# Output and gate weight pairs made beside the late convolution tiles, norm sums taken later, first squares queued behind the copies

## The chip, the cores and the metric

The kernel runs on one core of a Trainium2 chip. Five engines work side by side, each through its own queue in order: TensorE (PE, with PEld for its weight loads), VectorE (DVE), ScalarE (ACT), GpSimd (POOL), and SyncE (SP), which here issues nearly all transfers. The metric is the device time of one execution in microseconds; lower is better.

## The reference, cut to what matters

One layer over 2048 positions of width 1024, all in float32, and a final norm:

```python
h = rmsnorm(x, norm_g)
c_b, c_c, c_h, c_z, q, k, v, a_z = split(h @ w_in)         # 1024 x 4096
y_c = c_b * causal_dwconv(c_c * c_h, conv_w, conv_b)        # three taps
y_a = stick_breaking_attention(q, k, v)                     # 8 heads of 64
y = group_rmsnorm(concat(y_c, y_a)) * silu(concat(c_z, a_z))
x = x + y @ w_out                                           # 1024 x 1024
gate = sigmoid(rmsnorm(x, ple_norm_g) @ w_pg + b_pg)        # 1024 x 1024
x = x + gate * (p @ w_pe)
out = rmsnorm(x, final_g)
```

Stick-breaking attention takes, for a row of scores z, sigmoid(z) times the running product of sigmoid(-z) over the keys between key and query.

## The kernel before

The sequence lies in four chunks of 512 positions, c = 3, 2, 1, 0 (reversed, so chunk 3 needs no other). A weight tile is 128 output channels by 1024 inputs: eight blocks kt of 128x128, in two halves f of 128x512. Every float32 operand is split into a high part (a cast to the fast matmul type) and a low part (the rest), and a product is three matmuls: high by high, high by low, low by high (`product`, L283 to L285).

**Weights.** A half is either raw or a pair. A raw half is loaded into one of two `wr` buffers (`fetch_w`, L252, which loads as far ahead as the two buffers allow), cast on ACT to `wh` (L269), and the rest is taken on POOL as `wl` (L270). A half that another pass will need is then stored as a pair in DRAM (`store_w`, L277), and the later pass loads the pair (L266) with no work on ACT or POOL. Which halves are pairs is said by `paired`, which are stored by `kept`. The 16 output and gate tiles (`OUT0` and up) are raw and stored in the pass of chunk 3, pairs in those of chunks 2 and 1, and raw again in that of chunk 0.

**Order.** The program is traced in this order: the start (`first_tile` of tiles 24 and 16, for chunks 3 and 2, with the split of x and the first two norms); E, the projections of chunks 3 and 2; L, the projections of chunks 1 and 0 (q, k, v and attention gates first, then the convolution tiles c, h, b and g); `work2`, the last convolution tile with its gate; then for each chunk an output stage (`out_stage`, 8 tiles) and a gate stage (`gate_stage`, 8 tiles). A step is one `product`. Beside the steps runs `attention()`, pulled at a set rate per step (0.64 in E, 0.86 in L, 0.72 in the stages after), and generators called `besides`, one `next` per step: `norm_later`, `y_prep`, `final`, and `pe_pairs`, which splits and stores the eight tiles of w_pe. `later(n, f)` calls f n steps on. A scheduler then orders each engine's queue, so that work which it takes to be ready early can be issued ahead of what was traced before it; `tc.issue_after(ins)` holds what a block puts on the engine of `ins` behind `ins` in that queue, and no other engine's.

**Norms.** A norm is: squares summed over eight tiles into `acc`; `norm_r`, matmuls of `acc` by ones into `ssp` (L177); a DVE instruction (L183); a power on POOL (L185); then `norm_spread`, transposes into `rT` (L195) and a copy `rB` (L197) by which results are multiplied. At the start `first_squares` squares tiles 2, 4 and 6 and sums them on POOL (L206, L208), squares the others on ACT (L212), and the sums of these are DVE additions (L215). After a stage `out_stage` calls `norm_of` 6 steps on and `norm_spread` 10 steps on; `final` waits 8 steps, then calls `norm_of`, and 8 more before `norm_spread`.

**Attention.** A row: scores `z` (L535, L536), two ACT sigmoids (L538, L540), a DVE scan (L554, L557), a product on DVE or POOL in turn (L564), transposes `tp` (L603), a cast `ah` on ACT (L606), the rest `al` on DVE (L611), and two matmuls into `av` (L574, L575).

Single buffers that matter here (`BUFS`): `sh`, `sl` and `acc` have one each. PSUM tag `mm` has two banks, which the projections and stages share.

Of the kernel before, what the change touches and what calls it, by code (L numbers as in the profile page):

```python
# [14 lines left out]
P = 128  # L15
# [18 lines left out]
def build(tc, xt_d, pt_d, wst_d, wpe_d, cst_d, out_d):  # L34
# [5 lines left out]
    with ctx:  # L40
# [108 lines left out]

        latest = [None]  # L150

# [4 lines left out]
        def scaled_split(key, kt, xt, gain, lag=0):  # L156
            hh, hl = pair(key, kt)
            nc.scalar.activation(hh, xt, AF.Copy, scale=gain)

            def low():  # L160
                nc.vector.scalar_tensor_tensor(  # L161
                    out=hl, in0=xt, scalar=gain, in1=hh.bitcast(F32), op0=ALU.mult, op1=ALU.subtract)
                note()
            if lag:
                later(lag, low)
            else:
                low()
# [13 lines left out]
        def norm_sum(slot, ssp):  # L181
            r, r2 = rr[:, 8 * slot:8 * slot + 4], rr[:, 8 * slot + 4:8 * slot + 8]
            nc.vector.tensor_scalar(out=r, in0=ssp[:, 0:8:2], scalar1=1.0 / DM, scalar2=EPS,  # L183
                                    op0=ALU.mult, op1=ALU.add)
            nc.gpsimd.tensor_tensor(out=r, in0=r, in1=nhalf[:, 0:4], op=ALU.pow)  # L185
            if slot < 4:
                nc.vector.scalar_tensor_tensor(out=r2, in0=r, scalar=1.0 / HD, in1=r, op0=ALU.mult,
                                               op1=ALU.mult)
# [48 lines left out]
        def paired(t, tag):  # L237

            return tag[1] in (1, 2) if t >= OUT0 else tag == 1

        def kept(t, tag):
            return tag[1] == 3 if t >= OUT0 else tag == 3

        def fetch_w():

            while len(raws) < RAWS and fetched[0] < 2 * len(wq):
                t, tag = wq[fetched[0] // 2]
                f = fetched[0] % 2
                fetched[0] += 1
                if not paired(t, tag):  # L250
                    raw = pj.tile([P, CH], F32, tag="wr", bufs=RAWS, name=f"wr{t}_{made[0]}")
                    nc.sync.dma_start(raw, wst_d[t, f])  # L252
                    raws.append(raw)
# [33 lines left out]
        def proj(t, chunks, evac, besides=(None, None)):  # L287

            tag = chunks[0]
            for i, c in enumerate(chunks):  # L290
                pp = bank("mm", 2, f"pp{t}_{c}")
                for kt in range(KT):
# [7 lines left out]
                    yield  # L300
                if i and besides[i] is not None:
                    for _ in besides[i]:
                        pass
# [154 lines left out]

        def conv_c(ct, chunks):
            def evac(c, pp):  # L460
                cc[c] = buf("cc", f"cc{ct}_{c}")
                nc.vector.tensor_tensor(out=cc[c], in0=pp, in1=rB[c], op=ALU.mult)
                nc.gpsimd.tensor_tensor(out=cc[c], in0=cc[c], in1=rB[c], op=ALU.mult)

            return proj(4 + ct, chunks, evac)

        def conv_h(ct, chunks):
            def evac(c, pp):
# [17 lines left out]

            return proj(8 + ct, chunks, evac)

# [6 lines left out]

        def conv_b(ct, chunks):
            return proj(ct, chunks, evac_b(ct))

# [224 lines left out]
        def out_stage(c, besides=None):  # L723
# [26 lines left out]
            if besides is not None:  # L750
                for _ in besides:
                    yield
            later(6, norm_of, slot, ("x1", c))
            later(10, norm_spread, slot)

# [129 lines left out]
        def final(c):  # L885

            for _ in range(8):
                yield
# [64 lines left out]
        def pairs_of(chunks, order, last=None, first_besides=None):  # L953
# [3 lines left out]
            for n, (kind, i) in enumerate(order):  # L957
                besides = (first_besides if n == 0 else None, last if n == len(order) - 1 else None)
                if kind in kinds:
                    t0, f = kinds[kind]  # L960
                    args = (i, chunks) + ((besides,) if kind in "qv" else ())
                    add(work, f, *args, tiles=[(t0 + i, chunks[0])])
                else:
                    t, gi = (12 + i, i) if kind == "g" else (28 + i, 4 + i)
                    b = besides
                    if chunks == cE and (kind, i) in (("g", 1), ("g", 2)):
                        b = (norm_later(cL[i - 1]),) * 2
                    if chunks == cL and (kind, i) in (("g", 0), ("g", 1)):
                        b = (pairs_e,) * 2
# [28 lines left out]

        wq.extend([(24, cE[0]), (16, cE[0])])
        workE = pairs_of(cE, orderE, last=ahead(splits(1), 2))  # L1000
        pairs_e = pe_pairs()
        workL = pairs_of(cL, orderL[:-2], first_besides=ahead(splits(0), 2))
# [36 lines left out]
        split_w(att, ("ah", "al"))  # L1039
        adds3, acc3 = first_squares(3, x3)  # L1040
        for kt in range(KT):
            x_split(2, kt, x2[kt])
            if kt == 5:
                behind_first = latest[0]
        with tc.issue_after(behind_first):
            for f in adds3:
                f()
        first_tile(16, 3)
        norm_r(3, acc3)
        adds2, acc2 = first_squares(2, x2)  # L1050
        split_w()

        def beside_first(kt):
            if kt == 4:
                norm_spread(3)
            if kt == 6:
                evacs[24](3, pps[24, 3])
                evacs[16](3, pps[16, 3])
                tick()
        first_tile(24, 2, beside_first)  # L1060
        for f in adds2:
            f()
        split_w()
        first_tile(16, 2, lambda kt: tick() if kt in (2, 4, 6) else None)
        norm_r(2, acc2)
# [20 lines left out]
        for c in (3, 2, 1, 0):  # L1086
# [5 lines left out]
            def gates(c=c):  # L1092
                return gate_stage(c, y_prep(c - 1) if c else None)
            add(tail[-1], gates, need=[(h, c - 1) for h in range(NH)] if c else [],
                tiles=[(GATE0 + m, ("x1", c)) for m in range(KT)])
        run(workL, RATE_L)
        run(work2, RATE_Y)
        for work in tail[:3]:
# [70 lines left out]
```

## Time and profile before

| | |
|---|---|
| median of 3 runs | 1659.58 us (1654.53 to 1660.13) |
| the profiled execution | 1655.82 us, span 1654.1 us |
| mean granted TensorE clock | 0.981 |
| busy share | PE 96%, PEld 78%, DVE 69%, ACT 48%, POOL 46% |
| DMA | 333.99 MB, 202 GB/s over the span |

The span is from the first to the last instruction. The stages lie at: start 0 to about 62 us, E to 498, L to about 1025 (its convolution tiles from about 790), `work2` to 1058, output and gate stage of chunk 3 to about 1225, of chunk 2 to about 1420, of chunk 1 to about 1540, of chunk 0 to the end. A granted clock of 1 is full speed, 0.5 is half. A busy PE is modelled from pipelined matmuls, so a stage is judged by how much of it PE is not busy and by the clock it was granted.

### The profile page before, as it was taken

The page shows a single profiled execution, that of the slowest core. Times are in us where ns is not written, and L with a number is a line of the kernel's source. Part 1 is how long each engine was busy: PE and PEld are TensorE (multiplying, and loading weights), DVE is VectorE, ACT ScalarE, POOL GpSimd, SP SyncE. Part 2 cuts the span into 40 slices and gives each one's busy share as a digit, 9 for nine tenths or more (in the row PEclk, how much of TensorE's full clock was granted, in tenths as well). Part 3 has the DMA queues.
Part 4 walks back from the last instruction along what each step waited for, and adds up shares of the span by engine and source line. Part 5 has one row for each costly group of instructions (what it writes and reads, how often), then busy time and mean ns, then how long its engine had stood idle before and what let it go on. Part 6 is the DMA issues. An engine that isn't in the chain of part 4 may idle for free.

```text
span 1654.1 us, 23295 instructions
## 1 busy us (share of the span) xinstructions
PE 1589.9 (96%) x7622; PEld 1288.5 (78%) x7622; DVE 1145.1 (69%) x1475; ACT 796.8 (48%) x1574; POOL 757.8 (46%) x711
## 2 busy tenths in 40 slices
PE   7899999999999999999999999988999999999996
PEld 5778787887888788888888888767777777877885
DVE  6475677776655767666777777778877876854544
ACT  5344454554434545545444454456555454543453
POOL 7444545454460423223433432767664355424542
PEclk9899999999999999999999999998999999999998
DMA  6666766848547655556743333587877866868742
GB/s 215 196 213 187 242 200 204 263 136 255 196 160 230 203 149 186 160 182 193 230 136 110 125 117 108 162 278 268 281 262 259 282 225 229 277 201 289 246 133 89
DMA packets 184712, 333.99 MB, mean 202 GB/s; under 512 B 21776, under 2 KB 22800, under 8 KB 184592
## 3 DMA queue, kind: packets, MB, share of 16 engines
q1 hardware_dynamic: 181712, 327.27, 61.4%
q10 hardware_dynamic: 2880, 5.24, 0.9%
q8 instruction: 60, 0.98, 0.3%
q14 instruction: 60, 0.49, 0.1%
HBM read 217.08 MB, written 115.34 MB: 201 GB/s over the span
## 4 chain that ended last, share of the span: by engine, by line
PE 55%; DVE 5%; DMA 5%; POOL 4%; issue 3%; ACT 3%; SPq 1%; DVEq 0%; ACTq 0%; POOLq 0%
PE pp L283 8%; PE pp L284 8%; PE pp L285 8%; PE tp L603 4%; PE px L283 3%; PE px L285 3%; PE px L284 3%; PE z L535 2%; PE z L536 2%; PE av L575 2%; PE av L574 2%; PE py L283 2%; PE py L284 2%; PE py L285 2%; DVE T L557 2%
## 5 line engine op out<-in xcount | busy, mean ns | idle before, releaser
L283 PE MATMUL pp<-hhh,wh 128*128 128x512 f32 x1008 | 404.6, 401 | 0.0
L284 PE MATMUL pp<-hhl,wh 128*128 128x512 f32 x1008 | 398.5, 395 | 3.7 <-DVE hhl L161 3.6
L285 PE MATMUL pp<-hhh,wl 128*128 128x512 f32 x1008 | 397.1, 394 | 0.0
L557 DVE TENSOR_TENSOR_SCAN T<-s,carry,small 128x513 f32<-128x513 f32 x192 | 287.8, 1500 | 124.7 <-ACT s L538 116.5
L538 ACT ACTIVATE s<-z 128x512 f32<-128x512 f32 (+1 forms) x320 | 171.6, 536 | 272.3 <-PE z L536 269.9
L564 POOL TENSOR_TENSOR b<-b,T 128x512 f32<-128x512 f32 (+1 forms) x160 | 199.1, 1245 | 154.0 <-DVE T L557 66.9
L611 DVE TENSOR_TENSOR al<-tp,ah 128x512 fp32r<-128x512 f32 (+1 forms) x320 | 190.9, 597 | 46.1 <-ACT ah L606 45.6
L284 PEld LDWEIGHTS pp<-hhl,wh 128*128 128x128 f32 x1008 | 190.4, 189 | 41.5 <-DVE hhl L161 6.6
L285 PEld LDWEIGHTS pp<-hhh,wl 128*128 128x128 f32 x1008 | 189.9, 188 | 42.2
L270 POOL TENSOR_TENSOR wl<-wr,wh 128x512 fp32r<-128x512 f32 x126 | 178.7, 1420 | 95.7 <-ACT wh L269 85.4
L562 POOL COPY carry<-T 128x1 f32<-128x1 f32 x192 | 53.6, 279 | 363.4 <-DVE T L554 184.4
L283 PEld LDWEIGHTS pp<-hhh,wh 128*128 128x128 f32 x1008 | 190.3, 189 | 36.3 <-issue 1.0
L606 ACT CAST ah<-tp 128x512 fp32r<-128x512 f32 (+1 forms) x320 | 168.0, 526 | 83.9 <-PE tp L603 80.0
L603 PE MATMUL tp<-first,b 128*128 128x128 f32 x1088 | 174.5, 275 | 7.0 <-POOL b L564 3.8
L554 DVE TENSOR_TENSOR_SCAN T<-s,first 128x513 f32<-128x513 f32 (+3 forms) x128 | 125.5, 989 | 75.1 <-ACT s L538 71.7
L603 PEld LDWEIGHTS tp<-first,b 128*128 128x128 f32 x1088 | 138.4, 142 | 49.4 <-POOL b L564 4.8
L540 ACT ACTIVATE b<-z 128x512 f32<-128x512 f32 (+1 forms) x320 | 170.2, 532 | 0.0
L574 PE MATMUL av<-ah,vv 128*128 128x512 f32 (+1 forms) x320 | 140.8, 440 | 5.1 <-ACT ya L584 3.3
L564 DVE TENSOR_TENSOR b<-b,T 128x512 f32<-128x512 f32 (+2 forms) x160 | 131.4, 821 | 12.2 <-ACT ah L606 0.5
L535 PE MATMUL z<-kk,q 128*128 128x512 f32 (+1 forms) x320 | 119.7, 374 | 8.5 <-DMA kk<-qk_d 5.2
L269 ACT CAST wh<-wr 128x512 fp32r<-128x512 f32 x126 | 78.7, 624 | 88.7 <-DMA wr<-in_wst_dram 33.0
L575 PE MATMUL av<-al,vv 128*128 128x512 f32 (+1 forms) x320 | 118.9, 372 | 0.2 <-DVE al L611 0.2
(167 smaller groups left out, 2659.0 us busy)
## 6 DMA issues: line engine op xcount, KB each, us to landing
wr<-in_wst_dram SPq DMA_DIRECT2D x128, 256.0 KB, 3.1
wh<-wp_d SPq DMA_DIRECT2D x128, 256.0 KB, 3.1
wl<-wp_d SPq DMA_DIRECT2D x128, 256.0 KB, 3.5
wp_d<-wh SPq DMA_DIRECT2D x94, 256.0 KB, 3.4
wp_d<-wl SPq DMA_DIRECT2D x94, 256.0 KB, 3.6
kk<-qk_d SPq DMA_DIRECT2D x80, 256.0 KB, 4.2
vv<-v_d SPq DMA_DIRECT2D x80, 256.0 KB, 3.6
q<-qk_d SPq DMA_DIRECT2D x64, 256.0 KB, 4.3
```

Of the source, the lines that this page charges most:

```text
L270: nc.gpsimd.tensor_tensor(out=wl, in0=raw, in1=wh.bitcast(F32), op=ALU.subtract)
L283: nc.tensor.matmul(pp, wh[:, sl], hh, start=(kt == 0), stop=False)
L284: nc.tensor.matmul(pp, wh[:, sl], hl, start=False, stop=False)
L285: nc.tensor.matmul(pp, wl[:, sl], hh, start=False, stop=(kt == KT - 1))
L538: nc.scalar.activation(s[:, 1:w + 1], zp[:, 0:w], AF.Sigmoid, scale=-0.125)
L540: nc.scalar.activation(bt[:, 0:w], zp[:, 0:w], AF.Sigmoid, scale=0.125)
L557: nc.vector.tensor_tensor_scan(T[:, 0:w + 1], s[:, 0:w + 1], zeros.to_broadcast([P, w + 1]), carries[h, qc][:, j:j + 1], op0=ALU.mult, op1 ...
L564: return lambda: eng.tensor_tensor(out=bt[:, 0:w], in0=bt[:, 0:w], in1=T[:, 0:w], op=ALU.mult)
L574: nc.tensor.matmul(av[:, 0:w], v[:, kb], ah[:, 0:w], start=diag and kb == 3, stop=False)
L603: nc.tensor.transpose(tp[:, j * P:(j + 1) * P], bt[:, kb * P - k0:(kb + 1) * P - k0], ident)
L606: nc.scalar.copy(ah[:, 0:w], tp[:, 0:w])
L611: nc.vector.tensor_tensor(out=al[:, 0:w], in0=tp[:, 0:w], in1=ah[:, 0:w].bitcast(F32), op=ALU.subtract)
```

## The change

- `weight_pairs`, a new generator, makes all 32 halves of the output and gate tiles into pairs: it loads a raw half into `wr`, casts it into `sh` on ACT two steps on, takes the rest into `acc` on POOL, stores both four steps later, and yields once more, so that a half takes seven steps. It runs beside the 14 convolution and convolution gate tiles of L (224 steps). The output and gate tiles of chunks 3, 2 and 1 are then loaded as pairs; chunk 0's stay raw; none is stored in a stage. It runs on from tile to tile instead of being emptied at a tile's end, and what is left after L is drained.
- `pe_pairs` moves from the convolution gates 0 and 1 to the attention gates 1 and 2 of L, and also runs on.
- `fetch_w` looks no further than three halves past the last one made.
- `out_stage`: `norm_of` after 8 steps (was 6), `norm_spread` after 13 (was 10). `final`: 11 steps (was 8).
- The start: `first_squares(3)` is traced after the splits of chunk 2 and its ACT part queued behind the third of these copies; `norm_r(3)` comes six steps later, inside tile 24 of chunk 2; the POOL part of `first_squares(2)` is queued behind the power of norm 3; `norm_spread(3)` and the evacuations of chunk 3 move into tile 16 of chunk 2.

```diff
         def paired(t, tag):
-            return tag[1] in (1, 2) if t >= OUT0 else tag == 1
+            return tag[1] > 0 if t >= OUT0 else tag == 1
         def kept(t, tag):
-            return tag[1] == 3 if t >= OUT0 else tag == 3
+            return t < OUT0 and tag == 3
+        def weight_pairs():
+            for t in range(OUT0, OUT0 + 2 * KT):
+                for f in range(2):
+                    raw = pj.tile([P, CH], F32, tag="wr", bufs=RAWS, name=f"wr{t}_p{f}")
+                    nc.sync.dma_start(raw, wst_d[t, f])
+                    for _ in range(2):
+                        yield
+                    wh, wl = buf("sh", f"wh{t}_p{f}", F32R), buf("acc", f"wl{t}_p{f}", F32R)
+                    nc.scalar.copy(wh, raw)
+                    nc.gpsimd.tensor_tensor(out=wl, in0=raw, in1=wh.bitcast(F32), op=ALU.subtract)
+                    for _ in range(4):
+                        yield
+                    store_w(t, f, wh, wl)
+                    yield
         def fetch_w():
-            while len(raws) < RAWS and fetched[0] < 2 * len(wq):
+            while len(raws) < RAWS and fetched[0] < min(2 * len(wq), made[0] + 3):
...
-                if i and besides[i] is not None:
+                if i and besides[i] not in (None, pairs_w, pairs_e):
                     for _ in besides[i]:
                         pass
...
-            later(6, norm_of, slot, ("x1", c))
-            later(10, norm_spread, slot)
+            later(8, norm_of, slot, ("x1", c))
+            later(13, norm_spread, slot)
...
         def final(c):
-            for _ in range(8):
+            for _ in range(11):
                 yield
             norm_of(8 + c, ("o", c))
...
+                    if chunks == cL and kind in "chb":
+                        besides = (pairs_w,) * 2
+                    add(work, f, i, chunks, besides, tiles=[(t0 + i, chunks[0])])
...
-                    if chunks == cL and (kind, i) in (("g", 0), ("g", 1)):
+                    if chunks == cL and kind == "g":
+                        b = (pairs_w,) * 2
+                    if chunks == cL and kind == "a" and i in (1, 2):
                         b = (pairs_e,) * 2
...
-        adds3, acc3 = first_squares(3, x3)
         for kt in range(KT):
             x_split(2, kt, x2[kt])
+            if kt == 2:
+                copied = latest[1]
             if kt == 5:
                 behind_first = latest[0]
+        with tc.issue_after(copied):
+            adds3, acc3 = first_squares(3, x3)
         with tc.issue_after(behind_first):
             for f in adds3:
                 f()
         first_tile(16, 3)
-        norm_r(3, acc3)
-        adds2, acc2 = first_squares(2, x2)
-        split_w()
+        adds2 = []
         def beside_first(kt):
-            if kt == 4:
+            if kt == 5:
+                norm_r(3, acc3)
+                power = latest[2]
+                with tc.issue_after(power):
+                    adds2.extend(first_squares(2, x2))
+                split_w()
+        first_tile(24, 2, beside_first)
+        adds2, acc2 = adds2
+        def beside_second(kt):
+            if kt == 2:
                 norm_spread(3)
-            if kt == 6:
+            if kt == 3:
                 evacs[24](3, pps[24, 3])
                 evacs[16](3, pps[16, 3])
+                for f in adds2:
+                    f()
+                split_w()
+            if kt > 4:
                 tick()
-        first_tile(24, 2, beside_first)
-        for f in adds2:
-            f()
-        split_w()
-        first_tile(16, 2, lambda kt: tick() if kt in (2, 4, 6) else None)
+        first_tile(16, 2, beside_second)
         norm_r(2, acc2)
...
         run(workL, RATE_L)
+        for g in (pairs_e, pairs_w):
+            for _ in g:
+                tick()
```

`latest[1]` is set to the ACT copy in `scaled_split`, `latest[2]` to the POOL power in `norm_sum`; `conv_c`, `conv_h` and `conv_b` pass `besides` on to `proj`.

## Rows read from the trace of the kernel before

**Rows 1.** Page, part 1: busy us, share of the span, instructions
```profile
PE 1589.9 (96%) x7622; PEld 1288.5 (78%) x7622; DVE 1145.1 (69%) x1475; ACT 796.8 (48%) x1574; POOL 757.8 (46%) x711
```

**Rows 2.** Windows by stage: busy us (instructions), clock, DMA share, GB/s
```profile
core 0: us, PE busy (x) PEld busy (x) DVE busy (x) ACT busy (x) POOL busy (x), PEclk, DMA share, GB/s
100.00:498.00 398.00, 393.28 (x1954) 325.43 (x1953) 271.60 (x366) 189.43 (x399) 203.59 (x168) 1.00 0.64 204
498.00:790.00 292.00, 288.74 (x1435) 237.29 (x1434) 198.63 (x263) 143.62 (x288) 83.67 (x103) 1.00 0.61 188
...
830.00:1058.00 228.00, 227.76 (x1120) 184.90 (x1120) 171.55 (x232) 107.59 (x212) 93.26 (x99) 1.00 0.37 118
1058.00:1225.00 167.00, 153.74 (x696) 119.80 (x695) 134.16 (x141) 92.50 (x180) 123.53 (x102) 0.95 0.80 267
1225.00:1420.00 195.00, 186.68 (x886) 149.69 (x886) 149.94 (x182) 100.26 (x198) 84.86 (x85) 0.97 0.76 252
```

**Rows 3.** Windows of the start, columns as in rows 2
```profile
7.30:18.30 11.00, 7.34 (x26) 3.96 (x25) 10.62 (x9) 11.00 (x20) 10.00 (x7) 1.00 0.97 356
...
30.80:47.20 16.40, 7.87 (x24) 6.29 (x25) 7.57 (x8) 3.54 (x6) 13.53 (x16) 0.59 0.44 160
```

**Rows 4.** Timeline of PE in the start: start, us, [idle before <-releaser]
```profile
34.22 1.87 PE L177 MATMUL ssp<-small,xsq 128*128 128x2 f32 x8 [3.45 <-DVE xsq L215]
...
43.54 1.12 PE L195 MATMUL rT<-first,rr 128*128 128x128 f32 x4 [5.11 <-POOL rr L185]
```

**Rows 5.** Timeline of DVE in the start
```profile
36.13 0.16 DVE L183 TENSOR_SCALAR rr<-ssp 128x4 f32<-128x4 f32 x1 [0.29 <-PE ssp L177]
```

**Rows 6.** Timeline of POOL in the start
```profile
25.09 4.50 POOL L206 TENSOR_TENSOR xsq<-xf 128x512 f32<-128x512 f32 x1 [4.54 <-DVE xsq L215]
29.66 1.28 POOL L208 TENSOR_TENSOR xsq<-xsq,xsq 128x512 f32<-128x512 f32 x1
...
42.46 1.03 POOL L185 TENSOR_TENSOR rr<-rr,small 128x4 f32<-128x4 f32 x1
```

**Rows 7.** POOL by line, 1058 to 1225: busy us, mean ns | idle before
```profile
L270 POOL TENSOR_TENSOR wl<-wr,wh 128x512 fp32r<-128x512 f32 x30 | 45.6, 1521 | 8.4 <-ACT wh L269 8.4
```

**Rows 8.** ACT by line, 1058 to 1225
```profile
L269 ACT CAST wh<-wr 128x512 fp32r<-128x512 f32 x29 | 18.2, 627 | 16.1 <-DMA wr<-in_wst_dram 14.5 <-PE px L284 1.0 <-PE py L284 0.5
```

**Rows 9.** Waits of SP's queue, 1058 to 1225: us, times, longest
```profile
SPq L252 <- POOL wl L270: 42.2, 20, 5.8
```

**Rows 10.** Waits of PE, 1058 to 1250
```profile
PE ssp L177 <- POOL acc L717: 3.6, 2, 2.2
...
PE z L535 <- ACT b L540: 3.2, 2, 2.9
...
PE av L574 <- ACT ah L606: 1.7, 1, 1.7
```

**Rows 11.** Waits of PE, whole span
```profile
PE ssp L177 <- POOL acc L717: 7.5, 6, 2.6
```

**Rows 12.** Tiles py and px, high matmuls: first and last start
```profile
L283 PE MATMUL py<-yhh,wh x256: 387/390/796, 1058.3 to 1581.0; 128*128 128x512 f32 x128
...
L283 PE MATMUL px<-x1hh,wh x256: 387/392/774, 1139.4 to 1637.4; 128*128 128x512 f32 x128
```

**Rows 13.** DVE by line, 830 to 1058
```profile
L557 DVE TENSOR_TENSOR_SCAN T<-s,carry,small 128x513 f32<-128x513 f32 x43 | 62.6, 1456 | 33.9 <-ACT s L538 30.1 <-POOL b L564 2.6 <-POOL carry L562 0.6
...
L564 DVE TENSOR_TENSOR b<-b,T 128x512 f32<-128x512 f32 (+2 forms) x29 | 19.3, 664 | 2.1 <-ACT ah L606 0.5
```

**Rows 14.** DVE by line, 1058 to 1225
```profile
L557 DVE TENSOR_TENSOR_SCAN T<-s,carry,small 128x513 f32<-128x513 f32 x24 | 41.7, 1738 | 8.8 <-ACT s L538 8.8
...
L564 DVE TENSOR_TENSOR b<-b,T 128x512 f32<-128x512 f32 (+2 forms) x16 | 18.0, 1123 | 0.9
```

**Rows 15.** Window in chunk 1's output stage, columns as in rows 2
```profile
1425.00:1450.00 25.00, 25.00 (x122) 20.51 (x121) 23.57 (x29) 14.12 (x28) 9.53 (x12) 1.00 0.93 309
```

**Rows 16.** Waits of SP's queue, 830 to 1058
```profile
SPq L266 <- PE pp L285: 67.4, 22, 9.7
```

**Rows 17.** Page, part 6: transfers, KB each, us to landing
```profile
wp_d<-wh SPq DMA_DIRECT2D x94, 256.0 KB, 3.4
```

More of the change, by code (lines that the diff above doesn't have):

```diff
@@ L148, in load @@
             return t
-        latest = [None]
+        latest = [None] * 3
         def note():
@@ L158, in scaled_split @@
             nc.scalar.activation(hh, xt, AF.Copy, scale=gain)
+            latest[1] = nc.cur_bb.bb.instructions[-1]
             def low():
@@ L185, in norm_sum @@
             nc.gpsimd.tensor_tensor(out=r, in0=r, in1=nhalf[:, 0:4], op=ALU.pow)
+            latest[2] = nc.cur_bb.bb.instructions[-1]
             if slot < 4:
@@ L457, in build, with conv_c @@
         cc = {}
-        def conv_c(ct, chunks):
+        def conv_c(ct, chunks, besides=(None, None)):
             def evac(c, pp):
@@ L463, in evac, with conv_h @@
                 nc.gpsimd.tensor_tensor(out=cc[c], in0=cc[c], in1=rB[c], op=ALU.mult)
-            return proj(4 + ct, chunks, evac)
-        def conv_h(ct, chunks):
+            return proj(4 + ct, chunks, evac, besides)
+        def conv_h(ct, chunks, besides=(None, None)):
             def evac(c, pp):
@@ L485, in tap @@
                     op0=ALU.mult, op1=ALU.add)
-            return proj(8 + ct, chunks, evac)
+            return proj(8 + ct, chunks, evac, besides)
         def evac_b(ct):
@@ L494, in evac_b, with conv_b @@
             return evac
-        def conv_b(ct, chunks):
-            return proj(ct, chunks, evac_b(ct))
+        def conv_b(ct, chunks, besides=(None, None)):
+            return proj(ct, chunks, evac_b(ct), besides)
         jobs = [(h, c) for h in range(NH) for c in (3, 2)] + [(h, c) for c in (1, 0) for h in range(NH)]
@@ L960, in pairs_of @@
                     t0, f = kinds[kind]
-                    args = (i, chunks) + ((besides,) if kind in "qv" else ())
-                    add(work, f, *args, tiles=[(t0 + i, chunks[0])])
+                    if chunks == cL and kind in "chb":
+                        besides = (pairs_w,) * 2
+                    add(work, f, i, chunks, besides, tiles=[(t0 + i, chunks[0])])
                 else:
@@ L999, in build @@
         wq.extend([(24, cE[0]), (16, cE[0])])
+        pairs_e, pairs_w = pe_pairs(), weight_pairs()
         workE = pairs_of(cE, orderE, last=ahead(splits(1), 2))
-        pairs_e = pe_pairs()
         workL = pairs_of(cL, orderL[:-2], first_besides=ahead(splits(0), 2))
```

## The prediction

> **What bounds the kernel now.** I read the page first: PE is busy for 1589.9 us and no other engine comes near [rows 1]. So the kernel can only lose time where PE stands or runs at half clock, and the question is where that happens. Windows by stage answer it [rows 2]. I count a stage's loss as its length less PE's busy time, plus the busy time multiplied by one minus the granted clock. E loses 398 - 393.28 = 4.7 us, the first part of L 3.3, the late convolution tiles 0.2. Chunk 3's stages lose 13.3 standing and 153.74 x 0.05 = 7.7 by the clock, 20.9 in 167 us; chunk 2's lose 8.3 + 5.6 = 13.9 in 195. In the start, 30.80 to 47.20 loses 8.5 standing and 7.87 x 0.41 = 3.2 by the clock: 11.8 [rows 3]. Then the waits say what PE stood for: in the start for a sum of squares (3.45) and for the spread of the first norm (5.11), released by POOL's power [rows 4]; behind the stages for `acc` [rows 10, 11], and in chunk 3 for ACT.
>
> The clock here has two levels, 1.2 and 2.4 GHz, and a window mean of 0.59 is a mix of them. In each stage with a mean below 1 PE had stood for microseconds just before, so a stall costs more than its own length.
>
> **The change part by part.** The sum is made against the profiled execution, 1655.82 us, whose span is 1654.1; the median shown is 3.8 higher, within the spread of the three runs (5.6).
>
> *Squares behind the copies (ACT).* From 7.3 to 18.3 PE stands 3.7 us. ACT is busy all of it, but DVE too for 10.62 of 11.00 [rows 3], so copies that come sooner find DVE full of low parts. Nothing, with 3.7 gained and 1 lost (squares later than the additions that need them) as ends.
>
> *The first norm.* It now comes inside tile 24 of chunk 2, and only POOL's squares of chunk 2 are held behind its power. Before, the DVE step was over at 36.29, and the power ran at 42.46 [rows 5, 6]: 6.2 of the 8.5 us came from POOL's order alone, as POOL was then on other work (13.53 of 16.40 busy [rows 3]). The other 3.45 came from DVE's order, where a sum for chunk 3 stood behind additions for chunk 2; these are now traced after it. Upper end 11.8 gained. Lower end: the second norm becomes late instead. POOL's three squares and two sums for chunk 2 can't start before the power; at the undisturbed 1.28 us of one [rows 6] they are 6.4 us, so PE may stand some 6 us more in front of the second sum. I take **-8**, nearest to 6.2 and its share of the half clock (6.2/8.5 x 11.8 = 8.6).
>
> *Weight pairs, in chunk 3's stages.* 32 casts of 627 ns (20.1 us of ACT) and 32 subtractions of 1521 ns (48.7 us of POOL) leave [rows 7, 8], with 32 raw loads and 64 stores; 64 loads of pairs come. What the raw halves hold up is seen in two queues. SP stands 42.2 us at `wr` loads that wait for POOL to free a buffer [rows 9], and every transfer behind waits with them; ACT stands 14.5 us in front of casts whose half has not landed [rows 8], and the sigmoids and casts of attention stand behind. Two of PE's waits, for `ah` (1.7) and for a bank that ACT empties (3.2), follow these directly: 4.9, the lower end [rows 10]. For the upper end chunk 2's stages serve, which load pairs already: of their 13.9 lost, 2.2 [rows 10] and at most the rest of the sums' 7.5 [rows 11], 3.9, are norm waits, and the 5.6 of half clock I give to these; 2.2 are left, 1.9 for 167 us. Chunk 3, less its own norm wait of 1.4, would gain 20.9 - 1.4 - 1.9 = 17.6. I take the middle: **-11**. DVE profits too: its product took 1123 ns there against 664 in the late convolution tiles, its scan 1738 against 1456 [rows 13, 14].
>
> *Weight pairs, beside the late convolution tiles.* The same 32 casts, subtractions and 96 transfers now fall into a stretch that loses 0.2 us. POOL goes from 93.26 to some 142 of 228 us (62%), ACT from 107.59 to 128 [rows 2]. If DVE's 43 scans and 29 products stretched as far as in chunk 3's stages, that is 43 x 0.28 + 29 x 0.46 = 25 us, DVE at 197 of 228 (86%); a window with DVE at 94% had PE full [rows 15], so this is covered. SP is the weaker point: it already stands up to 9.7 us at pair loads waiting for PE [rows 16]. The stores and raw loads now queue there, and with one `sh` buffer the next cast waits for the store, 3.4 us to land [rows 17], three steps after its issue. Of steps of 1.27 us in chunk 3 (64 from 1058.3 to 1139.4 [rows 12]) that is 3.8: no margin when SP is blocked. Behind a waiting cast stand the sigmoids, and behind them DVE's scan and PE's transposes. Bounds: E, which makes raw halves all along, loses 4.7/398 per us, here 2.7; chunk 3's rate, 20.9/167, gives 28.5. E is nearer; for the single buffer I add 2: **+5**.
>
> I weigh a rule against this. POOL's square took 4.50 us where the undisturbed sum next to it took 1.28, so the two engines do hold each other up [rows 6], but in rows 13 and 14 only by part of an instruction. The Trainium skill (SBUF — State Buffer, "SBUF: two separate sides") says the shared port pair of VectorE and GpSimd is an exclusive lock, and that the loser fully blocks until the other's instruction ends. The 4.50 agrees, the means don't show it for every instruction; by the rule the late tiles' DVE would take all 48.7 us on top.
>
> *`pe_pairs` in the attention gates.* The same eight casts, subtractions and stores, in a part that loses 3.3 us of 292 [rows 2] and where `sl` is shared with q, k and v. Nothing to +3.3; I take **+1**. Its old place becomes free for the weight pairs.
>
> *Norm sums later.* Six waits for `acc`, 7.5 us, the longest 2.6 [rows 11], and the half clock of chunk 2's stages that I gave to them, 5.6: 13.1 at most. Two steps more are 2.5 us, three 3.8, about the longest wait. But the work traced in the added steps also lies in POOL's queue in front of the sum, so the wait may move with it: lower end nothing. I take **-7**, the middle. The spread three steps later is hidden by the first gate tile: its evacuation comes after some 14 steps, the spread after 13, and `mm` has a second bank; without that cover it would cost 3.8 us in each of four stages.
>
> *`fetch_w`'s limit, the drain, `besides` in the convolution tiles:* nothing; 224 steps hold 32 halves of seven, so the drain has nothing to do, and two raw halves are in flight as before (a late one at chunk 0's start would cost about a landing, 3.4 [rows 17]).
>
> Sum: -8 - 11 + 5 + 1 - 7 = -20; 1655.8 - 20 = **1636**.
>
> **The rivals.** *One, the start's wait only changes place*: PE stands for the second sum, as above. For it: five POOL instructions now start later. Against: the rest of tile 24, all of tile 16 and the next projection can be issued in front of it. The -8 is lost: 1644; at its worst 1650.
>
> *Two, the stages gain little*: what PE waits for there is DVE (134.16 of 167 busy [rows 2]), and raw halves cost only what follows directly, 4.9; the sums' waits move along. 1655.8 - 8 - 4.9 + 5 + 1 = 1649. Against: chunk 2's DVE is as busy (77%) and PE loses less.
>
> *Three, the other side: DVE becomes the bound of the late convolution tiles.* Each subtraction holds DVE for its whole length: 171.55 + 48.7 = 220 us. DVE's busiest stage reached 80%; at that ceiling the 228 us become 275, and the time 1655.8 - 26 + 1 + 47 = 1678. It outweighs the gains once the stretch passes 253 us, at 202 busy, so 31 us of added DVE time or 0.96 per subtraction. For it: the 4.50 us instruction. Against: the part-stretches, and 94% without loss [rows 15]. This is what the rule of the Trainium skill named above would do here.
>
> *Four, better*: all gains near their upper ends, 1655.8 - 11.8 - 17.6 - 13.1 + 2.7 = 1616.
>
> **How the numbers follow.** My sum 0.54, own range 1625 to 1647 (each of the three gains off by a third: 2.7, 3.7, 2.3, and the cost by 3); one 0.14; two 0.15; three 0.08; four 0.09. The predicted time is the first's. What a measurement of this kernel tells from no change is 0.5%, 8.3 us: faster means under about 1647.5. Faster: 0.53 of the first, four, 0.10 of one, 0.05 of two, 0.77. Slower: three. The rest, 0.15, is within. The range leaves out half of four below and three with a few per cent of one above: 1622 to 1656.
>
> **What would show it.** Start: the wait of 5.11 for `rr` gone, PE full from 18 to 60 at clock 1; wrong if PE stands at the second `ssp`. Chunk 3: no `wr` row for POOL there, SP's 42.2 gone, loss near 5 to 10 us. Late tiles: POOL near 60%, DVE under 90%, PE's loss under 8; wrong if ACT's casts stand microseconds for `wp_d` stores and PE's loss passes 25. Norms: PE's waits for `acc` under 3 us in all. The prediction is wrong above all if the late tiles give back what chunk 3 gains, or if the scheduler puts the first norm elsewhere.

## The result and the profile after

The median fell from 1659.86 us (1654.53 to 1661.66) to 1645.78 us (1643.53 to 1646.82): ratio 0.992, 95% interval 0.9903 to 0.9936. That is 10 us above the predicted 1636, inside the range, and faster by more than the 0.5% bound. The profiled execution took 1643.53 us, span 1641.8, against 1655.82 and 1654.1 before; by profiled executions, from which the sum was made, 12.3 us were gained where 20 were forecast. The profiled execution of the changed kernel is thus 7.5 above the forecast, and its median 2.3 above that.

The page of the changed kernel, part 1, answers to [rows 1]: PE is busy 7.1 us less, with the same 7622 matmuls.

```profile
PE 1582.8 (96%) x7622; PEld 1285.3 (78%) x7622; DVE 1147.1 (70%) x1475; ACT 796.2 (48%) x1574; POOL 758.2 (46%) x711
```

Its windows by stage (columns as in rows 2; E, first part of L, late convolution tiles, chunk 3's stages from their first output matmul to chunk 2's, then chunk 2's up to chunk 1's):

```profile
97.00:495.00 398.00, 393.98 (x1959) 326.56 (x1958) 272.15 (x367) 190.59 (x401) 205.29 (x168) 1.00 0.65 206
495.00:787.00 292.00, 288.63 (x1433) 237.05 (x1432) 201.24 (x262) 146.21 (x296) 90.73 (x110) 1.00 0.64 198
787.00:1072.00 285.00, 273.33 (x1316) 220.09 (x1316) 221.71 (x272) 137.73 (x274) 152.14 (x146) 0.98 0.62 206
...
1072.50:1225.30 152.80, 152.80 (x741) 122.71 (x740) 121.42 (x149) 81.35 (x159) 80.17 (x73) 1.00 0.75 248
1225.30:1387.90 162.60, 156.47 (x738) 124.03 (x737) 122.40 (x151) 82.46 (x162) 72.53 (x71) 0.98 0.75 251
```

For the stages of chunks 3 and 2 the same stretches of before, cut at the same matmuls (so chunk 3's end at 1234.5 and chunk 2's at 1398.5, not at the 1225 and 1420 by which the account of before goes), are these windows:

```profile
1058.30:1234.50 176.20, 162.94 (x741) 127.32 (x740) 140.23 (x150) 97.94 (x191) 126.83 (x105) 0.95 0.79 266
...
1234.50:1398.50 164.00, 157.17 (x738) 125.69 (x737) 126.44 (x151) 83.20 (x162) 72.58 (x72) 0.97 0.75 250
```

Chunk 3, with 741 PE instructions on both sides: 176.2 us became 152.8, with PE full and the clock at 1.00. Of the 23.4 us gained, 13.3 are time in which PE stood and 10.1 are matmuls that ran slower. In the late tiles it went the other way: PE was full there before [rows 2], now it stands 11.7 us and loses 273.33 x 0.02 = 5.5 by the clock.

Compared at the same matmul of each tile, the two traces give the account by stage. Single traces differ by a us or two in this: the changed kernel and the four below that keep its start as it is are 0.7 to 2.9 us ahead of the kernel before at 276 us.

| step | predicted | measured |
|---|---|---|
| start, with E's first part (to about 215 us) | -8 | -2.9 |
| first part of L (`pe_pairs`) | +1 | +0.3 |
| late convolution tiles | +5 | +16.8 |
| chunk 3's stages | -11 | -23.4 |
| chunk 2 to the end (norm sums) | -7 | -3.1 |
| sum | -20 | -12.3 |

The waits of PE over the whole span (us, times, longest), those that answer to [rows 4, 10, 11]:

```profile
PE av L593 <- ACT ya L603: 10.3, 3, 5.7
...
PE rT L197 <- POOL rr L186: 4.4, 1, 4.4
PE ssp L178 <- DVE xsq L217: 4.1, 2, 3.2
```

No wait of `ssp` for `acc` is left (7.5 before [rows 11]), and a new one leads the list: PE waits 10.3 us for ACT's copy of `av`, all of it in the late tiles.

**Where the late tiles stand.** ACT by line, 787 to 1050 (busy us, mean ns | idle before):

```profile
L557 ACT ACTIVATE s<-z 128x512 f32<-128x512 f32 (+2 forms) x66 | 36.3, 550 | 47.4 <-PE z L555 47.0 <-DVE u L489 0.3
...
L256 ACT CAST wh_p<-wr_p 128x512 fp32r<-128x512 f32 x32 | 19.9, 621 | 65.0 <-DMA wp_d<-wh_p 22.9 <-DMA wr_p<-in_wst_dram 14.3 <-POOL wl_p L257 11.0
```

32 casts cost 19.9 us of ACT, but ACT stands 65.0 us in front of them: for the store that frees `sh` (22.9), for the raw half to land (14.3), for POOL's subtraction, which also reads `sh` (11.0). The timeline of ACT, and then of PE, at the longest stall (start, us, [idle before <- releaser]):

```profile
870.68 0.62 ACT L256 CAST wh_p<-wr_p 128x512 fp32r<-128x512 f32 x1 [2.13 <-DMA wp_d<-wh_p]
...
875.23 0.62 ACT L256 CAST wh_p<-wr_p 128x512 fp32r<-128x512 f32 x1 [2.95 <-POOL wl_p L257]
...
876.26 0.58 ACT L602 COPY tmp<-av 64x512 f32<-64x512 f32 x1
876.85 0.58 ACT L603 COPY ya<-av 64x512 f32<-64x512 f32 x1
...
871.13 0.40 PE L303 MATMUL pp<-hhl,wh 128*128 128x512 f32 x1
871.36 0.40 PE L304 MATMUL pp<-hhh,wl 128*128 128x512 f32 x1
877.48 0.79 PE L593 MATMUL av<-ah,vv 128*128 128x512 f32 x1 [5.72 <-ACT ya L603]
878.08 0.63 PE L594 MATMUL av<-al,vv 128*128 128x512 f32 x1
878.50 0.63 PE L302 MATMUL pp<-hhh,wh 128*128 128x512 f32 x1
878.93 0.63 PE L303 MATMUL pp<-hhl,wh 128*128 128x512 f32 x1
```

The reader is to see the chain: two casts that are not ready stand in ACT's queue, the copies of `av` (L602, L603) stand behind them, and PE's next `av` needs that bank. PE stands 5.72 us; before the stall its matmuls started 0.23 us apart, behind it 0.43. The window behind the stall has PE full and a granted clock of 0.78, a mix of the two levels:

```profile
877.50:884.30 6.80, 6.80 (x24) 5.50 (x25) 5.28 (x6) 2.41 (x6) 5.20 (x3) 0.78 0.69 232
```

A second such stall follows 49 us later:

```profile
926.53 0.79 PE L593 MATMUL av<-ah,vv 128*128 128x512 f32 x1 [3.61 <-ACT ya L603]
```

All 32 casts lie within 163 us, 5.2 us apart, though `weight_pairs` asks for one in seven steps (held to their steps, as below, they come 7.2 us apart): the scheduler put them into ACT's queue ahead of their steps. The tile's row (min/median/max ns, first and last start):

```profile
L256 ACT CAST wh_p<-wr_p x32: 618/622/625, 787.1 to 949.8; 128x512 fp32r<-128x512 f32 x32
```

**The start.** Timelines of PE and POOL, answering to [rows 4, 6]:

```profile
31.11 1.87 PE L178 MATMUL ssp<-small,xsq 128*128 128x2 f32 x8 [3.22 <-DVE xsq L217]
...
42.31 1.02 PE L178 MATMUL ssp<-small,xsq 128*128 128x2 f32 x8 [0.86 <-DVE xsq L217]
...
49.96 1.12 PE L197 MATMUL rT<-first,rr 128*128 128x128 f32 x4 [4.43 <-POOL rr L186]
...
33.26 1.03 POOL L186 TENSOR_TENSOR rr<-rr,small 128x4 f32<-128x4 f32 x1 [6.95 <-DVE rr L184]
...
45.73 1.40 POOL L1111 TENSOR_SCALAR_AFFINE_SELECT draft<-draft 128x512 f32<-128x512 f32 x2
47.10 1.26 POOL L366 TENSOR_TENSOR sl<-qk,sh 128x512 fp32r<-128x512 f32 x1
48.31 0.61 POOL L1115 CAST sel<-draft 128x512 fp32r<-128x512 f32 x1
48.88 1.03 POOL L186 TENSOR_TENSOR rr<-rr,small 128x4 f32<-128x4 f32 x1
```

The first norm's power now runs as soon as its input is there (33.26), and nobody waits for it. But the second norm's power, whose input DVE delivers at 43.5, comes at 48.88, behind low parts and the making of `sel` (`draft`, L1111 to L1115), and PE stands 4.43 us for that one. The wait for the first sum still costs 3.22. At a matmul near 85 us the changed kernel is only 0.9 us ahead; the rest of the 2.9 comes between there and 215 us, and no run shows why.

### The profile page after: what moved, and what is told of

The parts are those of the page before. It is cut to its first block, busy times and chain, and to the rows that moved or that the text cites. A ratio compares the mean times of both kernels' runs of the same rounds, so it can differ in the third digit from the quotient of the medians.

```text
span 1641.8 us, 23384 instructions
## 1 busy us (share of the span) xinstructions
PE 1582.8 (96%) x7622; PEld 1285.3 (78%) x7622; DVE 1147.1 (70%) x1475; ACT 796.2 (48%) x1574; POOL 758.2 (46%) x711
## 4 chain that ended last, share of the span: by engine, by line
PE 43%; DVE 4%; DMA 3%; ACT 1%; issue 1%; POOL 1%; SPq 0%; DVEq 0%; ACTq 0%; POOLq 0%
PE px L302 4%; PE tp L622 4%; PE px L304 3%; PE px L303 3%; PE pp L302 3%; PE pp L303 3%; PE pp L304 3%; PE py L302 2%; PE py L303 2%; PE py L304 2%; PE av L594 2%; PE av L593 2%; PE z L554 2%; PE z L555 2%; DVE T L576 2%
## 5 line engine op out<-in xcount | busy, mean ns | idle before, releaser
L581 POOL COPY carry<-T 128x1 f32<-128x1 f32 x192 | 57.7, 300 | 320.6 <-DVE T L573 159.4
L289 POOL TENSOR_TENSOR wl<-wr,wh 128x512 fp32r<-128x512 f32 x94 | 131.7, 1404 | 84.7 <-ACT wh L288 74.3
L593 PE MATMUL av<-ah,vv 128*128 128x512 f32 (+1 forms) x320 | 140.3, 438 | 10.3 <-ACT ya L603 10.3
L554 PE MATMUL z<-kk,q 128*128 128x512 f32 (+1 forms) x320 | 119.2, 373 | 7.1 <-DMA kk<-qk_d 6.1
L555 PE MATMUL z<-kk,q 128*128 128x512 f32 (+1 forms) x320 | 118.0, 369 | 0.0
```

Of the source, the lines that this page charges most:

```text
L554: nc.tensor.matmul(zp[:, 0:w], q1[:, qs], K[n][:, k0:CH], start=True, stop=False)
L593: nc.tensor.matmul(av[:, 0:w], v[:, kb], ah[:, 0:w], start=diag and kb == 3, stop=False)
```

## The experiments

Each kernel ran beside the kernel before on the same chip; ratios are to that. "Stage" is chunk 3's, from its first `py` matmul to chunk 2's.

### Which part brings what

The three parts were run alone: the pairs with the old start and the old norm steps; the start alone; the steps of the norm sums alone. The core of the last, on the kernel before:

```diff
-            later(6, norm_of, slot, ("x1", c))
-            later(10, norm_spread, slot)
+            later(8, norm_of, slot, ("x1", c))
+            later(13, norm_spread, slot)
...
-            for _ in range(8):
+            for _ in range(11):
```

The pairs alone are the changed kernel with the old steps of the sums and the whole old start put back; the start alone is the kernel before with the diff's part from `first_tile(24, 3)` on and `latest`.

> The weight pairs (with the moved pe_pairs, the fetch limit and the drain) on the old start and the old places of the norm sums. If the parts add up: the late convolution tiles lose some 17 us as in the changed kernel and chunk 3's stages gain some 18 to 20, so 2 to 6 us faster than before, about 1655. Rival, that the pairs are what made the kernel faster and the sums nothing: 10 us or more faster, under 1650.

> The new start alone. If the start's wait only changed its place: 2 to 4 us faster than before, PE still standing 3 us for the first sum and 4 for the power of the second norm. Rival, that the start is worth the 8 us forecast and the rest of the changed kernel hides it: 7 to 9 us faster.

> Only the later norm sums (8, 13 and 11 steps). If these waits were real losses: 5 to 9 us faster, and PE's waits for acc go from 7.5 us to under 2. Rival, that the wait moves along with the work in front of it: within 2 us, waits for acc still 5 us or more.

| | median us | ratio | 95% interval |
|---|---|---|---|
| pairs alone | 1648.95 | 0.9954 | 0.9941 to 0.9967 |
| start alone | 1657.56 | 1.0003 | 0.9992 to 1.0015 |
| sums alone | 1652.98 | 0.9977 | 0.9965 to 0.9988 |

The parts add up to 11 us, near the 13 of the whole. The pairs carry it, with the same two sides: their late tiles lose 15.5 us and their stage takes 153.0, with the old norm steps too. They gain 7.6 us, between the 2 to 6 expected and the rival's 10. The start alone brings nothing that this can measure, less than the 2 to 4 expected: it trades the power's wait of 5.1 for 2.8 at the second norm, and the waits for the sums rise from 3.5 to 4.6. With the sums alone PE's waits for `acc` are gone (7.5 to 0), yet only 3.8 us come back, less than the 5 to 9 expected and more than the rival's 2; its stage for chunk 3 is no shorter (178.8).

### What the late tiles lose: the order on ACT, or the single buffer

On the changed kernel, each cast was held behind the newest sigmoid traced, so that it can't be queued ahead of its step:

```diff
             nc.scalar.activation(bt[:, 0:w], zp[:, 0:w], AF.Sigmoid, scale=0.125)
+            latest[3] = nc.cur_bb.bb.instructions[-1]
...
-                    nc.scalar.copy(wh, raw)
+                    with tc.issue_after(latest[3]):
+                        nc.scalar.copy(wh, raw)
```

> The changed kernel with each ACT cast of weight_pairs queued behind the latest sigmoid of attention traced before it, so that the 32 casts can't be issued ahead of their steps. If ACT's casts, standing in front of attention's work for a raw load or for the store that frees sh, cost the late tiles their 17 us: PE stands under 4 us there, and the time falls by 9 to 15 us against the changed kernel, to 1631 to 1637. Rival, that POOL's subtractions slowing DVE, or the transfers, cost it: the same work is only spread, and the time stays within 4 us of 1646.

1627.64 us, ratio 0.9823 (0.981 to 0.9835). Windows of the late tiles and of the stage, ACT's row of the casts from 787 to 1050, and the tile's row:

```profile
787.00:1057.00 270.00, 270.00 (x1331) 219.94 (x1330) 219.33 (x275) 139.93 (x277) 152.13 (x147) 1.00 0.65 219
...
1057.40:1210.20 152.80, 152.80 (x741) 122.76 (x740) 121.59 (x149) 81.47 (x159) 80.16 (x73) 1.00 0.75 248
```

```profile
L257 ACT CAST wh_p<-wr_p 128x512 fp32r<-128x512 f32 x32 | 20.0, 625 | 0.8 <-POOL carry L583 0.8
```

```profile
L257 ACT CAST wh_p<-wr_p x32: 619/622/644, 789.5 to 1012.4; 128x512 fp32r<-128x512 f32 x32
```

The same casts, subtractions, stores and buffers, and PE is full: ACT's 65.0 us in front of casts became 0.8, and the casts spread over 223 us. The late tiles now cost nothing, and the time fell by 18 us (16 by the ratios), more than the 9 to 15 expected. The edit sets the order and with it the pace; the two can't be told apart.

The rival was that the single buffer `sh` is short; here the pairs got a tag with more buffers and no order was held:

```diff
-                    wh, wl = buf("sh", f"wh{t}_p{f}", F32R), buf("acc", f"wl{t}_p{f}", F32R)
+                    wh, wl = buf("w1", f"wh{t}_p{f}", F32R), buf("w1", f"wl{t}_p{f}", F32R)
```

> The changed kernel with the pairs made in the six w1 buffers, which are idle there, in place of the single sh and acc; the casts are not held. If the single buffer was what made the casts wait: the late convolution tiles lose under 5 us and the time falls to about 1632 or below, as in casts_paced. If the cause is that the casts are issued ahead of their steps in ACT's queue: they run ahead still further, now stand for the raw load and for POOL to free wr, and the late tiles still lose 8 us or more; about 1638 to 1650.

1642.62 us, ratio 0.9908 (0.989 to 0.9926). ACT's row of the casts, 787 to 1050:

```profile
L256 ACT CAST wh_p<-wr_p 128x512 fp32r<-128x512 f32 x30 | 18.7, 622 | 44.9 <-DMA wr_p<-in_wst_dram 35.9 <-issue 5.6 <-POOL gg L433 2.0
```

The wait for the store is gone, but ACT stands in front of the casts all the same, now for raw halves, PE waits 10.5 us for `ya`, and the late tiles lose 14.1 us, 2.7 less than with one buffer. The 32 casts still come ahead of their steps, from 781.8 to 940.3. So in the main it is the order: a cast that is queued too early waits for whatever comes last.

### The start: what stands before the second power

On the changed kernel, the making of `sel` on POOL was held behind the second power:

```diff
-        for j, (pattern, base) in enumerate((([[-1, 8], [0, 16]], 0),
+        with tc.issue_after(latest[2]):
+            for j, (pattern, base) in enumerate((([[-1, 8], [0, 16]], 0),
```

> The changed kernel with POOL's making of sel (the draft instructions) queued behind the power of the second norm. If that power is late because of what stands in front of it on POOL: it runs some 3 us sooner, PE's wait of 4.4 for rr falls to about 1, and 3 to 5 us are gained, 1641 to 1643. Rival, that the start's loss goes to the next wait (the sum of squares, or the first scores' transfer): within 1.5 us of the changed kernel.

1641.88 us, ratio 0.99 (0.9879 to 0.9922). The wait for `rr` is gone and the first scores come at 55.9, against 60.3 in the changed kernel; near 85 us this kernel is 5.1 us ahead of the kernel before, the changed kernel 0.9. But by 715 us the two are level again (2.4 and 2.9 ahead). The interval overlaps that of the changed kernel, so the gain in the whole is not shown by the times, only the wait's place by the trace.

Both edits together:

> casts_paced and sel_behind_power together, on the changed kernel. If the two don't touch: 1627.6 less 3 to 5, 1622 to 1625. Rival, that the start's gain is lost later: within 1.5 us of 1627.6.

1625.5 us, ratio 0.9798 (0.9776 to 0.982). In the trace this kernel is 5.6 us ahead of the kernel before at 715 us, the one with held casts 0.5; but the medians are 2.1 us apart and the interval overlaps that of held casts alone (0.981 to 0.9835), so neither expectation is settled.

Then the first sum, for which PE still stood 3.2 us, was taken four steps later, inside tile 16 (both edits above kept):

```diff
+            if kt == 1:
+                norm_r(3, acc3)
+                power = latest[2]
+                with tc.issue_after(power):
+                    more, acc = first_squares(2, x2)
...
-            if kt == 2:
+            if kt == 5:
                 norm_spread(3)
-            if kt == 3:
+            if kt == 6:
                 evacs[24](3, pps[24, 3])
```

> paced_and_sel with the first norm's sum four steps later in PE's trace (step 2 of tile 16 of chunk 2, its spread and evacuations three steps after that). If PE stands 3.2 us at that sum only because it is placed before its additions are done: this wait goes and 2 to 4 us are gained, to about 1622. Rival, that the wait moves to the second sum, whose POOL squares now start later still: within 1.5 us of paced_and_sel's 1625.5, or slower.

1622.86 us, ratio 0.9786 (0.9766 to 0.9805), not told apart from the run above. PE's two waits for sums of squares:

```profile
32.44 1.56 PE L178 MATMUL ssp<-small,xsq 128*128 128x2 f32 x8 [3.16 <-DVE xsq L217]
...
44.15 1.05 PE L178 MATMUL ssp<-small,xsq 128*128 128x2 f32 x8 [2.77 <-DVE xsq L217]
```

The wait for the first sum did not go (3.16 us, 3.23 in the run above): DVE's last addition for it came a microsecond later too. The wait for the second grew from 1.83 to 2.77. So the premise, that the sum was only placed too early, is not borne out. By its median this is the fastest kernel of the study, and its ratio lies clear of the changed kernel's 0.992 (0.9903 to 0.9936).

### What of the raw halves cost chunk 3's stages 23 us

Three suspects: POOL's load, which stretches DVE's work; SP's and ACT's waits for raw halves; the casts on ACT. First, POOL's load was put back by itself: on the kernel with held casts, 32 subtractions on a scratch tile (extra work, no part of the result), one for each pair loaded in chunk 3's stages.

```diff
+                    if t >= OUT0 and tag[1] == 3:
+                        with tc.issue_after(latest[4]):
+                            nc.gpsimd.tensor_tensor(out=scratch, in0=scratch, in1=scratch, op=ALU.subtract)
```

> casts_paced with one more POOL subtraction of 128x512 for each half of chunk 3's stages, on a scratch tile that nothing else reads, queued behind attention's latest carry copy: POOL's load of the raw halves comes back without their casts, loads, buffers or stores. If POOL's load, by slowing DVE and what stands behind it on POOL, was what those stages lost by: their loss goes from 0 to 10 us or more, the time from 1628 to 1638 or more. If the queues were (SP behind wr loads, ACT behind casts): the loss stays under 4 us and the time within 5 us of 1628.

1638.08 us, ratio 0.9868 (0.985 to 0.9886). Window of the stage, then lines of DVE and POOL from 1057 to 1211:

```profile
1059.00:1222.30 163.30, 156.06 (x742) 123.44 (x741) 134.82 (x149) 81.65 (x161) 120.84 (x103) 0.99 0.69 233
```

```profile
L583 DVE TENSOR_TENSOR_SCAN T<-s,carry,small 128x513 f32<-128x513 f32 x24 | 38.1, 1587 | 5.9 <-ACT s L563 5.9
...
L591 DVE TENSOR_TENSOR b<-b,T 128x512 f32<-128x512 f32 (+2 forms) x16 | 16.3, 1018 | 0.9
...
L291 POOL TENSOR_TENSOR scratch<-scratch 128x512 f32<-128x512 f32 x30 | 35.0, 1166 | 0.4
```

The same two lines of DVE with held casts and no scratch work, from 1057 to 1201:

```profile
L578 DVE TENSOR_TENSOR_SCAN T<-s,carry,small 128x513 f32<-128x513 f32 x24 | 34.7, 1444 | 10.5 <-ACT s L558 9.3 <-POOL rr L186 1.2
...
L585 DVE TENSOR_TENSOR b<-b,T 128x512 f32<-128x512 f32 (+2 forms) x16 | 12.4, 776 | 0.9
```

POOL's load alone takes back 10.5 of the 23.4 us: the stage goes from 152.8 to 163.3, the product from 776 to 1018 ns, the scan from 1444 to 1587. POOL is busy 120.84 us there against 126.83 before, so this is a little less load than the real one. It reaches PE by more than one way: of the 7.2 us that PE stands, 3.1 are for DVE's `al`, 3.4 for ACT and 0.4 for POOL's `acc`, and POOL's own products of 128x512 take longer too (1705 ns in the mean against 1311). How much of it goes through DVE alone is not shown.

Second, a third `wr` buffer in the kernel before, to take the waits for raw halves away and leave the work:

```diff
-        RAWS = 2
+        RAWS = 3
```

> The kernel before with three wr buffers in place of two. In chunk 3's stages the raw halves then block SP and ACT less, while POOL makes as many subtractions. If the waits in those two queues were what chunk 3's stages lost by: their loss of 21 us falls by half or more and the kernel gains 8 us or more. If POOL's load on DVE was: the loss stays above 15 and the time within 5 us of before.

1653.79 us, ratio 0.9969 (0.9957 to 0.9982); the stage took 172.8 us, 3.4 less. ACT's 14.5 us of waits for raw halves are gone, so by themselves they were worth no more than about these 3.4. SP's waits for POOL to free a buffer are still there (42.2 before [rows 9]):

```profile
SPq L252 <- POOL wl L270: 46.0, 19, 5.8
```

Third, in the kernel before, the casts of raw output and gate halves were held behind the newest sigmoid, as the pairs' casts were above:

```diff
-                    nc.scalar.copy(wh, raw)
+                    with (tc.issue_after(latest[1]) if t >= OUT0 else ExitStack()):
+                        nc.scalar.copy(wh, raw)
```

> The kernel before with each ACT cast of a raw output or gate half queued behind the latest sigmoid of attention traced before it. POOL's load and SP's waits stay. If ACT standing in front of casts was a good part of what chunk 3's stages lost by: ACT's 14.5 us of waits for wr fall below 5 and 4 to 10 us are gained. If POOL's load and SP's queue were nearly all of it: within 3 us of before.

1657.42 us, ratio 1.0003 (0.9993 to 1.0013). ACT's waits in the stage:

```profile
ACT wh L270 <- DMA wr<-in_wst_dram: 15.9, 10, 5.2
```

It is inconclusive: the order was held, but ACT still stands for halves that have not landed (14.5 before [rows 8]), and PE waits 5.7 us for `wl` in addition. So the edit did not take away what it was to test.

## Why the prediction was right, and where its steps were not

The direction and the range held, but in part by luck, as errors of both signs met: late tiles 12 worse and start 5 worse than forecast, norm sums 4 worse, chunk 3 12 better. Without either of the two errors of 12 us the time would have been about 1634 or 1658.

**Start, -8: failed.** The step that the first norm's power was held up by POOL's order alone was right (33.26 instead of 42.46), and so was the test that the wait of 5.11 would go. Its size was read wrongly: 6.2 us is how late the power was, and of the 8.5 us that PE stood only 5.11 were for it; with its share of the half clock that is 5.1/8.5 x 11.8 = 7.1, not 8.6. The step that priced the lower end failed: rival one came true, with another cause than it named. I let PE stand for the second *sum*; it stands 0.86 there, and 4.43 for the second *power*, behind `sel`, which I had not listed among the work that POOL would have in front of it; holding `sel` back took the wait away. And the 3.45 for the first sum, which I gave to DVE's order, is 3.22. The squares' place on ACT did help from 7.3 to 18.3, where PE had stood 3.7 us [rows 3] and is now busy for all 11.00, but from 18.3 to 30.8 it fell from 12.47 us busy to 7.65, in front of the sum (2.9) and of low parts that DVE makes (1.9); so "nothing" stands.

**Chunk 3's stages, -11: right mechanism, the term too small by 12.** Its signs all came: no `wr` work there, SP's 42.2 gone, PE's loss 0 where I had said 5 to 10. The step that failed is the choice of the middle, and the upper end of 17.6 itself, as it left a residue of chunk 2's kind; the whole loss went, 13.3 standing and 10.1 of slower matmuls. I had priced DVE's profit as an aside; by the scratch work POOL's load, on DVE and in POOL's own queue, is the largest single piece found, 10.5 us. In the kernel before, a third buffer bought 3.4, which need not add to these 10.5. How the rest divides between SP's waits, the 20 us of casts on ACT and the heavier subtraction stays open, since the run that was to show ACT's share didn't remove its wait. The lower end, 4.9, was low from the start: PE's longest wait in this stage before was one that I did not count, 3.3 us for ACT's copy of `av`, the wait that leads the list in the late tiles after:

```profile
PE av L574 <- ACT ya L584: 3.3, 1, 3.3
```

**Late convolution tiles, +5: failed, 16.8.** The weak point was named rightly (a cast that waits, with the sigmoids behind it) and the sign to look for came, "ACT's casts stand microseconds for `wp_d` stores". But I charged it to the single buffer and to SP, at 2 us, on the premise that a cast comes in its step. The cause is that the scheduler issues casts ahead of their steps; more buffers gave back 2.7 us, holding the order all of it. What PE stood for was not what follows the sigmoids but the copies of `av`, whose one bank PE needs next. That the scheduler can issue work ahead of what was traced before it stands in the account of the kernel; I used it for the start, and not here.

**Rival three** needed DVE to take each subtraction's whole length. With held casts DVE is busy 219.33 of 270 us and PE stands nowhere, against 204.45 of 273 in the same tiles of before, by this window:

```profile
787.00:1060.00 273.00, 272.76 (x1341) 221.55 (x1340) 204.45 (x275) 127.77 (x256) 112.57 (x125) 1.00 0.43 137
```

That is 15 us more, not 48.7, and covered. What failed is the rival's size, not the blocking, which the means hide and single instructions show. Timelines of DVE and then of POOL in the scratch run (start, us):

```profile
1069.19 1.52 DVE L591 TENSOR_TENSOR b<-b,T 128x512 f32<-128x512 f32 x1
1070.63 2.29 DVE L583 TENSOR_TENSOR_SCAN T<-s,carry,small 128x513 f32<-128x513 f32 x1
...
1075.70 0.69 DVE L591 TENSOR_TENSOR b<-b,T 128x512 f32<-128x512 f32 x1
...
1084.24 1.28 DVE L583 TENSOR_TENSOR_SCAN T<-s,carry,small 128x513 f32<-128x513 f32 x1
...
1067.35 2.82 POOL L291 TENSOR_TENSOR scratch<-scratch 128x512 f32<-128x512 f32 x2
1070.12 1.72 POOL L439 TENSOR_TENSOR gg<-gg,cc 128x512 f32<-128x512 f32 x1
...
1074.48 6.33 POOL L471 TENSOR_TENSOR gr<-gr,small 128x32 f32<-128x32 f32 x1
```

A product that starts with 0.98 us of POOL's instruction left takes 1.52 us in place of 0.69; a scan that starts with 1.21 left takes 2.29 in place of 1.28. In this run's whole trace 34 of DVE's 96 products of 128x512 start inside a POOL instruction of 128x512 with over 0.25 us left, and each takes what is left plus 0.55 us; of the others none takes over 0.72. So the rule of the Trainium skill (SBUF — State Buffer, "SBUF: two separate sides"), that the loser fully blocks until the other engine's instruction ends, agrees with these instructions. It does not agree with the last line shown, a power on POOL over 128x32, which runs for 6.33 us with a DVE product of 0.69 us inside it. The step that failed in the rival is that each subtraction would cost DVE its whole length: DVE waits only for what is left of the instruction under way, and often none is. In the stage of the scratch run POOL's busy time rose by 120.84 - 80.16 = 40.7 us and DVE's by 134.82 - 121.59 = 13.2.

**Norm sums, -7: the mechanism right, the size half.** The waits for `acc` are gone, as the test wanted. What they cost was 3.8 us alone (interval 2.0 to 5.8) and 3.1 in the whole, not 7.5 and the half clock of chunk 2's stages that I gave to them; the pairs alone, with the old steps, gain 1.2 in the same stretch. Chunk 2's stages still stand 6.1 us (6.8 before) and run at 0.98 (0.97), with a new wait of 2.8 us for DVE's `al` among the rest.

**`pe_pairs`, +1:** +0.3, within what was bounded. The rest at nothing held.

## What to carry to other kernels

Work moved into a stage that has room is not free because the engine has room: where a scheduler may issue it early, it can stand unready in an in-order queue in front of work that is due, so tie each moved instruction to its step, and look for its idle time in front rather than its busy time. When a wait on a shared queue is removed, list everything that this queue will hold in front of the next urgent instruction, small setup work too. A stage that loses time to several causes at once can give back all of it when their common source leaves, more than each wait that is listed in it.

## What the runs showed of the hardware that was not expected

- A DVE product or scan that starts inside a large POOL instruction waits for what is left of that instruction (0.98 us left: 1.52 in place of 0.69), but a power of 128x32 on POOL did not hold it up. In the mean POOL's added work cost DVE about a third of its length: 13.2 us on 40.7 in chunk 3's stages, 15 on 39.6 (152.13 less 112.57) in the late tiles.
- DVE's busy share does not say by itself whether PE loses: 81% in the late tiles with held casts cost nothing, 83% in chunk 3's stages with scratch work cost 10.5 us.
- Behind the stall of 5.72 us matmuls started 0.43 us apart instead of 0.23, the lower of the clock's two levels; for 11.7 us of standing the late tiles lost 5.5 more by the clock.
